# Tying the value and MoBA score matmuls of two heads, and their transposes, into runs

## Chip, core and metric

The kernel runs on one core of a Trainium2 chip. The metric is device microseconds of one execution, as the median of several runs. Times below are in microseconds (us) unless marked ns.

## What is computed

A trunk of two layers over 256 tokens of width 1024. Each layer normalises and modulates its input, projects it, runs eight MoBA heads and eight NSA heads (64 wide each), gates them, projects back and adds the result. With 256 tokens, one MoBA block covers the whole sequence and every NSA block is selected, so a MoBA head is one causal attention and an NSA head is the sum of two (selected and window branch) and a small compressed one.

```python
# MoBA, for each head: own block only
s_own = einsum('hqd,hkd->hqk', q, k_own); s_own = where(d_own >= 0, s_own - slope*d_own, NEG)
p = softmax(s_own); o_m = einsum('hqb,hbd->hqd', p, v_own)
# NSA, for each head: three gated branches
o_n = g0 * softmax(s_c) @ vc + g1 * softmax(s_s) @ vs + g2 * softmax(s_w) @ vw
y = concat([o_m * silu(zm), o_n * silu(zn)]) @ w_out
```

## The kernel before

**Projections.** TensorE (PE) multiplies float32 in split form: VectorE (DVE) and ScalarE (ACT) turn each 128x1024 unit of weights into a high part (`split_hi`, the `hi` cast of L364) and a low part (`split_lo`, the `lo` subtraction of L372), and `mm3` (L399 to L401) issues three matmuls per product. These are the bulk of PE's work; most have 256 columns and use the whole 128x128 array. Raw units come by DMA on SyncE's (SP) queue into a pool `raw` of eight slots, and a slot is free again when its `lo` is done.

**Attention.** Work goes by blocks of two heads (j = 0, 1), four NSA and four MoBA blocks a layer. Each has scores on PE, `softmax` on DVE and ACT (bias and minimum L545, exponential L548, reciprocal L550, a scaling per span at L555 on ACT or L557 on DVE), three transposes of 128x128 per head and branch (`transposed`, L565), a copy of the transposes out of PSUM (`PT`, L570 on ACT or L568 on DVE), the value matmuls, and `gate_out`.

- `nsa_block`: per head two score tiles (L586, L587), four spans; then six transposes, branch by branch (i = 0 selected, 1 window). The value sums of both heads stand in one PSUM bank `av`, head 0 on partitions 0 to 63, head 1 on 64 to 127, so each value matmul uses all 128 rows of the array and 64 of its columns: `vx` by `pct` for the compressed branch (L596), 256 columns of queries for the first key tile (L602), 128 for the second (L604).
- `moba_block`: per head the scores of the first query tile (128x128, L615) and of the second (128x256, L617). They contract over 64 partitions, head 0 on rows 0 to 63 of the array, head 1 on rows 64 to 127, into one `sc` bank each. Value matmuls at L627 (256) and L630 (128).

A float32 matmul that is not split shows as two records in the trace, each over the same columns; a transpose shows as one.

**What sets the order.** `PLAN` lists the steps; a scheduler then orders each engine's instructions by readiness and by the place in the program, so that projection matmuls of later steps fill PE while a softmax is under way. Nothing in the program before says that two matmuls should stand next to each other. The start of the first layer (up to about 56 us) has its order written by hand.

**Pools.** `raw` 8 slots, `work` 3 (the probability tiles `S` come from it), `probT` 3 (the `PT` copies); PSUM banks `tr` 2 (transposes), `sc` 2 (scores), `av` 1.

Of the kernel before, what the change touches and what calls it, by code (L numbers as in the profile page):

```python
# [41 lines left out]
# The first layer's modulation and first projections: (first row block, number) of each stage.  # L42
STAGES = [(0, 1), (1, 1), (2, 2), (4, 2), (6, 2)]
# Per stage, the engine that rounds its first weights to float32r: 1 ScalarE, 2 VectorE.
HIGH_ENGINE = (1, 2, 2, 1, 1)
# Per stage, the units of the next stage's modulation summed on VectorE (the rest on TensorE).
ON_VECTOR = (0, 0, 2, 2)
# Per stage, the column blocks of its projection before which parts of the next stage's
# modulation go: (units on TensorE), sums, columns.
ADA_AT = [((1, 1), 2, 3), ((0, 0, 2, 2), 2, 3), ((6, 6), 6, 6), ((2, 5), 5, 6)]  # L50
# Matmuls that keep the array's clock up before and after silu(c) and before the projections.
WARM = (1, 13, 6)

# Order of the steps: layer, kind, index, and after a colon choices of engines:
# p: modulation on TensorE; d: high parts of weights on VectorE; t: one of two copies of
# transposed probabilities on VectorE; v, s: normalisation on VectorE, ScalarE only.
# [12 lines left out]
class Trunk:  # L69
    def __init__(self, tc, ins, out):  # L70
        self.tc = tc
        self.nc = tc.nc
        self.I = ins
        self.out = out
        self.depth = ins["w_ada"].shape[0]
        self.n = 0
        self.how = ""
        self.used = set()
        self.parts, self.pv, self.z = {}, {}, [None, None]
# [12 lines left out]
    # ---------------------------------------------------------------- setup  # L92
# [64 lines left out]
    def silu_c(self):  # L157
        """silu(c) as columns, and each as the first of 32 columns (the others zero)."""
        nc = self.nc
        pc = self.tl(self.ps, [P, 512], "tr", bufs=2)  # L160
        nc.tensor.transpose(pc[:, :KK], self.c8, self.ident[:KK, :KK])
        th = self.cp.tile([P, KK], F32, name="cth")
        nc.scalar.activation(th, pc[:, :KK], AF.Tanh, scale=0.5)
        self.cs = self.cp.tile([P, KK], F32, name="cs")
        nc.vector.scalar_tensor_tensor(out=self.cs, in0=th, scalar=1.0, in1=pc[:, :KK],
                                       op0=OP.add, op1=OP.mult)
        nc.vector.tensor_scalar_mul(self.cs, self.cs, 0.5)
        nc.vector.tensor_copy(self.csz[:, :, 0], self.cs)

    # ------------------------------------------------------------------ ada  # L170
# [6 lines left out]
    def mod_rows(self, bank=("tr", 2)):  # L177
        """Columns of b_ada (+1 on the scale part), g_pre and g_post of a layer."""
# [9 lines left out]
    def ada_loads(self, l, spec, slots=None):  # L188
        """Weights of 512 columns of the modulation; spec lists (part, first kk, n kk)."""
# [14 lines left out]
    def ada_on_pe(self, pm, spec, i, raw, done=0):  # L204
        """Unit i of a group: each column block sums over d on its own 32 array columns
        (a single block of each part on two of them, for even and odd row blocks)."""
# [41 lines left out]
    def ada_cols(self, spec, ev):  # L248
        """The sums as columns of self.mod, with the bias and the norm's weight."""
# [29 lines left out]
    def warm(self, n):  # L279
        """Matmuls whose result nobody reads, to keep the array's clock up."""  # L280
# [4 lines left out]
    def gate_rows(self):  # L285
        """The gate part as rows, the same on every partition (through DRAM)."""
# [11 lines left out]
    # -------------------------------------------------------------- helpers  # L298
    def rstd(self, a, b):
        """(sum of the two mean-square parts + eps) ** -0.5."""  # L300
# [48 lines left out]
    def load(self, pieces, nk, n):  # L349
        """DMA of column pieces side by side into one unit."""  # L350
# [25 lines left out]
    def split(self, unit, tags=None):  # L376
        """The two f32r parts of a unit (in slots of self.mp if tags are given)."""
        return self.split_lo(unit, self.split_hi(unit, tags), tags)
# [4 lines left out]
    def weights(self, w, cols, tags=()):  # L383
        """Both f32r parts of the columns, a list over the 8 row blocks."""
# [11 lines left out]
    def mm3(self, out, aH, aL, bH, bL, first, last):  # L396
        """out (+)= a.T @ b from f32r parts: low terms first."""
# [14 lines left out]
    def col_chunk(self, l, cols, evac, t=None):  # L412
        """A chunk with the weights stationary; for one token tile at a time if t is given."""
# [14 lines left out]
    # ----------------------------------------------------------- compression  # L428
    def compress_in(self, l, pj):
        """The key and value columns by place within a block, and the place embeddings."""  # L430
# [105 lines left out]
    # ------------------------------------------------------------- attention  # L536
    def softmax(self, sc, h, spans, w):
        """Normalised (and gated) probabilities of the score spans of one bank."""
# [14 lines left out]
        for i, (a, b) in enumerate(spans):  # L553
            if b - a > P and "v" not in self.how or "s" in self.how:
                nc.scalar.activation(s[:, a:b], s[:, a:b], AF.Copy, scale=sm[:, i:i + 1])  # L555
            else:
                nc.vector.tensor_scalar_mul(s[:, a:b], s[:, a:b], sm[:, i:i + 1])  # L557
        return s

    def transposed(self, blocks, alt):  # L560
        """Transposes of the three causal probability blocks of one head and branch."""
        nc = self.nc
        pt = self.tl(self.ps, [P, 512], "tr", bufs=2)
        for i, blk in enumerate(blocks):
            nc.tensor.transpose(pt[:, i * P:(i + 1) * P], blk, self.ident)  # L565
        ps = self.tl(self.pp, [P, 3 * P], "PT")
        if alt and "t" in self.how:
            nc.vector.tensor_copy(ps, pt[:, :3 * P])  # L568
        else:
            nc.scalar.copy(ps, pt[:, :3 * P])  # L570
        return ps

    def nsa_block(self, b):
# [3 lines left out]
        pts = []  # L577
        for j in range(2):
            h = 2 * b + j
            s01 = []  # L580
            for qt in range(NT):
# [8 lines left out]
            pts.append([self.transposed([s01[0][:, i * P:(i + 1) * P],  # L590
                                         s01[1][:, i * S:i * S + P],
                                         s01[1][:, i * S + P:(i + 1) * S]], i)
                        for i in range(2)])
        for j in range(2):
            h = 2 * b + j
            nc.tensor.matmul(av[j * HD:(j + 1) * HD, :S], self.vx[:, h, :], self.pct,  # L596
                             start=True, stop=False)
        for i in range(2):
            for j in range(2):
                o = av[j * HD:(j + 1) * HD, :]  # L600
                vc = slice(i * P + g * HD, i * P + (g + 1) * HD)
                nc.tensor.matmul(o[:, :S], self.vsw[:, 0, vc], pts[j][i][:, :S],  # L602
                                 start=False, stop=False)
                nc.tensor.matmul(o[:, P:S], self.vsw[:, 1, vc], pts[j][i][:, S:],  # L604
                                 start=False, stop=(i == 1))
        self.gate_out(av, 4 + b)

    def moba_block(self, b):
        nc = self.nc
        av = self.tl(self.ps, [P, 512], "av", bufs=1)  # L610
        pts = []
        for j in range(2):
            rows = slice(j * HD, (j + 1) * HD)
            sc = self.tl(self.ps, [P, 512], "sc", bufs=2)
            nc.tensor.matmul(sc[:, 0:P], self.qm[rows, b, 0:P], self.km[rows, b, 0:P],  # L615
                             start=True, stop=True)
            nc.tensor.matmul(sc[:, P:3 * P], self.qm[rows, b, P:S], self.km[rows, b, :],  # L617
                             start=True, stop=True)
            s = self.softmax(sc, 2 * b + j, [(0, P), (P, 3 * P)], None)
            pts.append(self.transposed([s[:, i * P:(i + 1) * P] for i in range(3)], j))  # L620
        for kt in range(2):
            for j in range(2):
                h = 2 * b + j
                o = av[j * HD:(j + 1) * HD, :]
                vc = slice(h * HD, (h + 1) * HD)
                if kt == 0:
                    nc.tensor.matmul(o[:, :S], self.vm[:, 0, vc], pts[j][:, :S],  # L627
                                     start=True, stop=False)
                else:
                    nc.tensor.matmul(o[:, P:S], self.vm[:, 1, vc], pts[j][:, S:],  # L630
                                     start=False, stop=True)
# [11 lines left out]
    # ---------------------------------------------------------------- output  # L643
# [8 lines left out]
    def out_mm(self, t):  # L652
        """Pieces (columns, bank) of y @ w_out for a token tile."""
# [43 lines left out]
    # ------------------------------------------------------------- evacuation  # L697
# [10 lines left out]
    def ev_k(self, pj):  # L708
        """High and low parts of the keys of both branches, on both halves of the partitions."""
# [16 lines left out]
    def ev_qn(self, i):  # L726
        """The NSA queries whole, and per head as high and low parts on the two halves."""
# [29 lines left out]
    # ------------------------------------------------------------------ layer  # L757
# [16 lines left out]
    def first_layer_start(self):  # L774
        """Modulation, h and the first projections, some of the 8 row blocks at a time."""
# [140 lines left out]
    def first(self, name, l):  # L916
        """Whether this is the first use of a tile in a layer."""
# [4 lines left out]
    def step(self, token):  # L922
        """One step of PLAN: layer, kind, index and, after a colon, engine choices."""
# [71 lines left out]
    def run(self):  # L995
        from contextlib import ExitStack
        with ExitStack() as self.stack:
            self.cp = self.pool("const")
            self.rp = self.pool("raw", bufs=8)
# [3 lines left out]
            self.wp = self.pool("work", bufs=3)  # L1003
            self.pp = self.pool("probT", bufs=3)
# [28 lines left out]
```

## Time and profile before

| | us |
|---|---|
| median of 3 runs | 355.85 |
| lowest and highest run | 354.7, 356.37 |
| span of the profiled execution | 354.4 |
| PE busy (96% of the span), 2852 matmul records | 341.4 |
| PEld (weight loads) | 299.6 |
| DVE busy (75%) | 266.1 |
| ACT busy (58%) | 204.3 |
| POOL | 10.5 |

The span of 354.4 is the one time that the profile has for its own execution; the runs' median is 1.45 above it. PE's busy time counts each matmul from its start to its modelled end, and these overlap: what a matmul holds PE for is read from its start to the start of the next. A projection matmul of 256 columns has a duration of 0.28 and its successor starts 0.12 after it. The granted clock of PE is 1.00 (2.4 GHz) in every stretch that matters here.

### The profile page before, as it was taken

What the parts mean: (1) busy time and instruction counts of PE and PEld (TensorE: products, weight loads), DVE (VectorE), ACT (ScalarE), POOL (GpSimd) and SP (SyncE); (2) the same over time, 40 slices, a digit from 0 to 9 for tenths busy, and PEclk for the clock granted to TensorE, in tenths of its full rate; (3) what the DMA queues carried; (4) which work ended last, traced back from release to release, by engine and by line L of the source; (5) the groups of instructions that cost most, each with busy time, mean ns of one, the idle gap of its engine ahead of it and who ended that gap; (6) DMA issues with size and microseconds to landing.
All of it is one profiled execution on the core that took longest, in us unless ns stands there. A gap on an engine that the chain in (4) does not pass through costs nothing.

```text
span 354.4 us, 7595 instructions
## 1 busy us (share of the span) xinstructions
PE 341.4 (96%) x2852; PEld 299.6 (85%) x2852; DVE 266.1 (75%) x727; ACT 204.3 (58%) x506; POOL 10.5 (3%) x23
## 2 busy tenths in 40 slices
PE   7999999999999999989999999999999999999993
PEld 7789889988887878767998999998878898677993
DVE  2648669999987898879898985999987646776132
ACT  4423407776989863757365455543889655668211
POOL 2000001100000000000011000000000000000000
PEclk9999999999999999999999999999999999999998
DMA  7999999939955566899755798489454330000111
GB/s 237 321 331 353 350 338 220 308 108 354 347 186 154 167 217 210 259 351 333 197 149 162 223 284 247 130 285 352 130 160 139 119 120 2 0 2 1 62 60 59
DMA packets 72060, 71.12 MB, mean 201 GB/s; under 512 B 11440, under 2 KB 61784, under 8 KB 72024
## 3 DMA queue, kind: packets, MB, share of 16 engines
q1 hardware_dynamic: 72024, 70.65, 64.1%
q8 instruction: 22, 0.36, 0.4%
q14 instruction: 14, 0.11, 0.1%
HBM read 69.58 MB, written 1.06 MB: 199 GB/s over the span
## 4 chain that ended last, share of the span: by engine, by line
PE 73%; DVE 13%; DMA 6%; issue 4%; ACT 2%; POOL 1%; SPq 1%; DVEq 0%; POOLq 0%; ACTq 0%
PE pj L399 13%; PE pj L400 13%; PE pj L401 13%; PE tr L565 5%; DVE lo L372 4%; PE av L602 3%; PE tr L216 3%; DMA yL<-in_w_ada_dram 2%; DMA raw<-in_w_out_dram 2%; PE av L627 2%; PE sc L586 2%; PE sc L617 2%; PE av L604 2%; PE pj L839 2%; PE av L596 2%
## 5 line engine op out<-in xcount | busy, mean ns | idle before, releaser
L372 DVE TENSOR_TENSOR lo<-raw,hi 128x1024 fp32r<-128x1024 f32 (+3 forms) x82 | 90.7, 1123 | 15.9 <-ACT hi L364 15.5
L399 PE MATMUL pj<-hH,lo 128*128 128x256 f32 x320 | 93.1, 291 | 0.0
L400 PE MATMUL pj<-hL,hi 128*128 128x256 f32 x320 | 92.5, 289 | 0.0
L401 PE MATMUL pj<-hH,hi 128*128 128x256 f32 x320 | 92.1, 288 | 0.0
L364 ACT CAST hi<-raw 128x1024 fp32r<-128x1024 f32 (+4 forms) x70 | 66.0, 966 | 22.7 <-PE pj L401 17.1
L399 PEld LDWEIGHTS pj<-hH,lo 128*128 128x128 f32 x320 | 61.0, 191 | 4.4 <-issue 3.4
L400 PEld LDWEIGHTS pj<-hL,hi 128*128 128x128 f32 x320 | 61.0, 191 | 2.2 <-issue 1.7
L401 PEld LDWEIGHTS pj<-hH,hi 128*128 128x128 f32 x320 | 61.0, 191 | 1.4 <-issue 1.1
L548 ACT ACTIVATE S<-S,mn 128x128 f32<-128x128 f32 (+1 forms) x96 | 42.7, 448 | 4.4 <-DVE mn L545 4.1
L233 DVE SCALAR_TENSOR_TENSOR acc<-raw,cs,acc 128x512 f32<-128x512 f32 x49 | 36.5, 747 | 1.6 <-DMA raw<-in_w_ada_dram 1.2
L545 DVE CUSTOM_DVE_ANT_0 S<-sc,bias 128x128 f32<-128x128 f32 (+1 forms) x96 | 31.6, 350 | 7.6 <-PE tr L565 3.1
L399 PE MATMUL pj<-hi,yL 128*128 128x256 f32 x112 | 31.9, 285 | 0.0
L401 PE MATMUL pj<-hi,yH 128*128 128x256 f32 x112 | 31.9, 286 | 0.0
L400 PE MATMUL pj<-lo,yH 128*128 128x256 f32 x112 | 31.8, 285 | 0.0
L565 PE MATMUL tr<-ident,S 128*128 128x128 f32 x144 | 29.6, 281 | 0.0
L570 ACT COPY PT<-tr 128x384 f32<-128x384 f32 x44 | 20.3, 478 | 10.0 <-PE tr L565 9.9
L565 PEld LDWEIGHTS tr<-ident,S 128*128 128x128 f32 x144 | 17.5, 140 | 6.7 <-issue 3.0
L555 ACT ACTIVATE S<-S,sm 128x256 f32<-128x256 f32 (+1 forms) x46 | 20.4, 483 | 2.9 <-DVE sm L550 1.4
L399 PEld LDWEIGHTS pj<-hi,yL 128*128 128x128 f32 x112 | 21.2, 189 | 0.9 <-issue 0.9
L401 PEld LDWEIGHTS pj<-hi,yH 128*128 128x128 f32 x112 | 21.1, 189 | 0.5 <-issue 0.5
L400 PEld LDWEIGHTS pj<-lo,yH 128*128 128x128 f32 x112 | 21.0, 188 | 0.3 <-issue 0.3
L548 ACT ACTIVATION_READ_ACCUMULATOR S<-S,mn 128x1 f32 x96 | 18.3, 190 | 0.0
(248 smaller groups left out, 650.1 us busy)
## 6 DMA issues: line engine op xcount, KB each, us to landing
raw<-in_w_in_dram SPq DMA_DIRECT2D x43, 512.0 KB, 4.5
raw<-in_w_ada_dram SPq DMA_DIRECT2D x32, 512.0 KB, 4.6
raw<-in_w_out_dram SPq DMA_DIRECT2D x16, 512.0 KB, 7.2
raw<-in_w_in_dram SPq DMA_DIRECT2D x9, 256.0 KB, 3.9
qs<-in_w_ada_dram SPq DMA_DIRECT2D x4, 512.0 KB, 7.2
yH<-in_w_ada_dram SPq DMA_DIRECT2D x4, 512.0 KB, 7.2
yL<-in_w_ada_dram SPq DMA_DIRECT2D x4, 512.0 KB
raw<-in_w_in_dram SPq DMA_DIRECT2D x9, 128.0 KB, 5.7
```

The costliest lines, as they stand in the source:

```text
L216: self.nc.tensor.matmul(pm[32 * r:32 * r + 32, :P], self.csz[:, k, :], raw[:, j, c * P:(c + 1) * P], start=first <= k < first + turns, sto ...
L233: nc.vector.scalar_tensor_tensor(out=out, in0=raw[:, j], scalar=self.cs[:, k:k + 1], in1=out, op0=OP.mult, op1=OP.add)
L364: self.nc.scalar.copy(hi[:, :nk * n], raw[:, :nk * n])
L372: self.nc.vector.tensor_sub(lo[:, :nk * n], raw[:, :nk * n], hi[:, :nk * n].bitcast(F32))
L399: nc.tensor.matmul(out, aL, bH, start=first, stop=False)
L400: nc.tensor.matmul(out, aH, bL, start=False, stop=False)
L401: nc.tensor.matmul(out, aH, bH, start=False, stop=last)
L545: nc.vector.tensor_tensor_reduce(out=s[:, a:b], in0=sc[:, a:b], in1=self.bias[:, h, S - (b - a):S], scale=-1.0, scalar=3.0e38, op0=OP.add, ...
L548: nc.scalar.activation(s[:, a:b], s[:, a:b], AF.Exp, bias=mn[:, i:i + 1], scale=-1.0, accum_out=sm[:, i:i + 1])
L555: nc.scalar.activation(s[:, a:b], s[:, a:b], AF.Copy, scale=sm[:, i:i + 1])
L565: nc.tensor.transpose(pt[:, i * P:(i + 1) * P], blk, self.ident)
L570: nc.scalar.copy(ps, pt[:, :3 * P])
```

## The change

The change touches only `softmax` (it now remembers its last instructions), `transposed`, `nsa_block`, `moba_block`, three pool sizes, and comments.

- A new helper `beside` gives every matmul of a list a wait on all instructions of a second list, and puts an order among the matmuls.
- The transposes of one branch of both heads are one list of six, and all six wait for the scalings of both heads (in an NSA block the eight scalings of the branch's spans are `scaled[i::2]`, four for each branch).
- The value matmuls of a branch are one list in the order head 0, head 1, head 0, head 1, and wait for both `PT` copies. In the selected branch the two `vx` matmuls stand at the head of the list.
- The four MoBA score matmuls of a block are one list in the order head 0, head 1 for 128 columns, then both for 256; the list waits for nothing more.
- `raw` has seven slots, `work` four, `probT` four.

```diff
-    def transposed(self, blocks, alt):
...
+    def transposed(self, pair, after):
+        nc = self.nc
+        mms, pts = [], []
+        for j, blocks in enumerate(pair):
+            pt = self.tl(self.ps, [P, 512], "tr", bufs=2)
+            mms += [nc.tensor.transpose(pt[:, i * P:(i + 1) * P], blk, self.ident)
+                    for i, blk in enumerate(blocks)]
+            ps = self.tl(self.pp, [P, 3 * P], "PT")
...
+        self.beside(mms, after)
+        return pts
+    def beside(self, mms, lasts):
+        for mm in mms:
+            for last in lasts:
+                self.tc.add_manual_dep(mm.ins, last.ins.name, mybir.DependencyInfo(
+                    mybir.DependencyClass.Sync, mybir.DependencyReason.DATA), reason="beside")
+        for a, b in zip(mms, mms[1:]):
+            self.tc.add_manual_dep(b.ins, a.ins.name, mybir.DependencyInfo(
+                mybir.DependencyClass.NoSync, mybir.DependencyReason.DATA), reason="order")
     def nsa_block(self, b):
...
+        scaled = self.scaled[-8:]
         for i in range(2):
+            pts = self.transposed([[s01[0][:, i * P:(i + 1) * P],
+                                    s01[1][:, i * S:i * S + P],
+                                    s01[1][:, i * S + P:(i + 1) * S]] for s01 in probs],
+                                  scaled[i::2])
+            mms = []
+            if i == 0:
+                mms += [nc.tensor.matmul(av[j * HD:(j + 1) * HD, :S], self.vx[:, 2 * b + j, :],
+                                         self.pct, start=True, stop=False) for j in range(2)]
...
+            for kt in range(2):
+                for j in range(2):
+                    mms.append(nc.tensor.matmul(
+                        av[j * HD:(j + 1) * HD, kt * P:S], self.vsw[:, kt, vc],
+                        pts[j][:, kt * S:S + kt * P], start=False, stop=(i == 1 and kt == 1)))
+            self.beside(mms, self.copies[-2:])
     def moba_block(self, b):
...
+        sc = [self.tl(self.ps, [P, 512], "sc", bufs=2) for _ in range(2)]
+        mms = []
+        for qt in range(2):
+            for j in range(2):
+                rows = slice(j * HD, (j + 1) * HD)
+                mms.append(nc.tensor.matmul(
+                    sc[j][:, qt * P:P + qt * S], self.qm[rows, b, qt * P:(qt + 1) * P],
+                    self.km[rows, b, :(qt + 1) * P], start=True, stop=True))
+        self.beside(mms[::1], [])
+        ss = [self.softmax(sc[j], 2 * b + j, [(0, P), (P, 3 * P)], None) for j in range(2)]
+        pts = self.transposed([[s[:, i * P:(i + 1) * P] for i in range(3)] for s in ss],
+                              self.scaled[-4:])
...
-            self.rp = self.pool("raw", bufs=8)
+            self.rp = self.pool("raw", bufs=7)
...
-            self.wp = self.pool("work", bufs=3)
-            self.pp = self.pool("probT", bufs=3)
+            self.wp = self.pool("work", bufs=4)
+            self.pp = self.pool("probT", bufs=4)
```

**How the order moves, place 1.** PE, the value matmuls of the second NSA block of layer 0. Before, they stand in four groups, of which the last three follow here; head 0 has `PT_1278` and `PT_1284` (selected and window branch), head 1 `PT_1318` and `PT_1324`.

```order
L565 MATMUL tr_1314<-ident,S_1289 128x128
L602 MATMUL av_1245<-PT_1278,vsw_169 64x256
L565 MATMUL tr_1320<-ident,S_1289 128x128
L604 MATMUL av_1245<-PT_1278,vsw_169 64x128
...
L602 MATMUL av_1245<-PT_1318,vsw_169 64x256
L604 MATMUL av_1245<-PT_1318,vsw_169 64x128
L602 MATMUL av_1245<-PT_1284,vsw_169 64x256
L604 MATMUL av_1245<-PT_1284,vsw_169 64x128
L602 MATMUL av_1245<-PT_1324,vsw_169 64x256
L604 MATMUL av_1245<-PT_1324,vsw_169 64x128
```

The same block with the change (selected branch; `PT_1306` is head 0, `PT_1312` head 1):

```order
L569 MATMUL tr_1302<-ident,S_1263 128x128 x2
L569 MATMUL tr_1308<-ident,S_1277 128x128
L569 MATMUL tr_1308<-ident,S_1291 128x128 x2
L402 MATMUL pj_1669<-hH_167,hi_1665 128x256
L569 MATMUL tr_1320<-ident,S_1249 128x128
L569 MATMUL tr_1320<-ident,S_1263 128x128 x2
L400 MATMUL pj_1784<-hH_167,lo_1776 128x256
L617 MATMUL av_1245<-pct_1076,vx_1049 64x256 x2
L622 MATMUL av_1245<-PT_1306,vsw_169 64x256
L622 MATMUL av_1245<-PT_1312,vsw_169 64x256
L622 MATMUL av_1245<-PT_1306,vsw_169 64x128
L622 MATMUL av_1245<-PT_1312,vsw_169 64x128
```

The ten value matmuls of a block go from four groups to two of six and four, heads alternating; between a branch's transposes and its value matmuls only a few other matmuls are left.

**Place 2.** PE, MoBA scores of layer 1, near the end of the NSA blocks. Before (`sc_4097` is head 1 of the first MoBA block, `sc_4125` and `sc_4144` the two heads of the second):

```order
L615 MATMUL sc_4097<-km_3546,qm_3545 128x128
L565 MATMUL tr_4051<-ident,S_4026 128x128
L602 MATMUL av_3982<-PT_4015,vsw_2460 64x256
...
L617 MATMUL sc_4097<-km_3546,qm_3545 128x256
L615 MATMUL sc_4125<-km_3546,qm_3545 128x128
...
L617 MATMUL sc_4125<-km_3546,qm_3545 128x256
...
L615 MATMUL sc_4144<-km_3546,qm_3545 128x128
L617 MATMUL sc_4144<-km_3546,qm_3545 128x256
```

Now (`sc_4125` and `sc_4126` are the two heads of the second block):

```order
L636 MATMUL sc_4125<-km_3546,qm_3545 128x128
L636 MATMUL sc_4126<-km_3546,qm_3545 128x128
L636 MATMUL sc_4125<-km_3546,qm_3545 128x256
L636 MATMUL sc_4126<-km_3546,qm_3545 128x256
L622 MATMUL av_3982<-PT_4061,vsw_2460 64x256
L622 MATMUL av_3982<-PT_4067,vsw_2460 64x256
L622 MATMUL av_3982<-PT_4061,vsw_2460 64x128
L622 MATMUL av_3982<-PT_4067,vsw_2460 64x128
```

The four scores of a block stand together here and in the third block of layer 1. In five of the other six blocks the first of the four still stands alone, with 1 to 9 other matmuls behind it; in the sixth the last one does. Before, layer 0 had all four scores of a block next to each other in each of its blocks, head after head; layer 1 had its sixteen scores in eleven groups.

**Place 3.** ACT, from the copies of the second NSA block's selected branch to those of the third, with the change:

```order
L575 COPY PT_1306<-tr_1302 128x384
L575 COPY PT_1312<-tr_1308 128x384
...
L575 COPY PT_1330<-tr_1326 128x384
L365 CAST hi_1872<-raw_1870 128x1024
L557 ACTIVATE S_1484<-S_1484,sm_1486 128x256 x2
...
L549 ACTIVATE S_1512,sm_1514<-S_1512,mn_1513 128x256 x2
L365 CAST hi_1878<-raw_1876 128x1024
L557 ACTIVATE S_1512<-S_1512,sm_1514 128x256 x2
L575 COPY PT_1527<-tr_1523 128x384
```

`S_1484` belongs to head 0 and `S_1512` to head 1 of the third block; the six transposes behind `PT_1527` wait for both now, and a `hi` cast stands ahead of the last scaling. Before, the transposes of head 0 waited for `S_1484` alone.

## Rows read from the trace of the kernel before

**Rows 1.** The page, chain that ended last, shares of the span by engine.

```profile
PE 73%; DVE 13%; DMA 6%; issue 4%; ACT 2%; POOL 1%; SPq 1%; DVEq 0%; POOLq 0%; ACTq 0%
```

**Rows 2.** Stages: us; busy (x instructions) of PE, PEld, DVE, ACT, POOL; clock; DMA.

```profile
94.00:134.00 40.00, 40.00 (x296) 31.70 (x293) 34.41 (x129) 32.42 (x97) 0.00 (x0) 1.00 0.63 196
...
243.00:280.00 37.00, 37.00 (x280) 30.15 (x280) 29.94 (x114) 29.95 (x88) 0.00 (x0) 1.00 0.50 165
296.00:330.00 34.00, 34.00 (x228) 24.48 (x226) 23.35 (x100) 23.71 (x75) 0.00 (x0) 1.00 0.01 1
```

**Rows 3.** Timeline of PE: start, duration, line, operands, records; value matmuls, layer 0.

```profile
101.47 0.28 PE L399 MATMUL pj<-hH,lo 128*128 128x256 f32 x1
101.68 0.66 PE L602 MATMUL av<-PT,vsw 128*64 128x256 f32 x4
102.16 0.40 PE L604 MATMUL av<-PT,vsw 128*64 128x128 f32 x4
102.38 0.59 PE L602 MATMUL av<-PT,vsw 128*64 128x256 f32 x2
102.81 0.38 PE L604 MATMUL av<-PT,vsw 128*64 128x128 f32 x2
103.12 0.44 PE L565 MATMUL tr<-ident,S 128*128 128x128 f32 x2
```

**Rows 4.** Timeline of PE: first groups of value matmuls of the second NSA block.

```profile
104.68 0.65 PE L596 MATMUL av<-pct,vx 128*64 128x256 f32 x4
105.26 0.39 PE L399 MATMUL pj<-hH,lo 128*128 128x256 f32 x1
105.48 0.28 PE L400 MATMUL pj<-hL,hi 128*128 128x256 f32 x1
105.60 0.27 PE L401 MATMUL pj<-hH,hi 128*128 128x256 f32 x1
...
107.56 0.65 PE L602 MATMUL av<-PT,vsw 128*64 128x256 f32 x2
108.13 0.33 PE L565 MATMUL tr<-ident,S 128*128 128x128 f32 x1
108.39 0.43 PE L604 MATMUL av<-PT,vsw 128*64 128x128 f32 x2
108.75 0.38 PE L586 MATMUL sc<-wide,qs 128*128 128x256 f32 x1
```

**Rows 5.** Timeline of PE: first group of value matmuls of a MoBA block.

```profile
162.53 0.65 PE L627 MATMUL av<-PT,vm 128*64 128x256 f32 x2
163.10 0.39 PE L399 MATMUL pj<-hi,yL 128*128 128x256 f32 x1
```

**Rows 6.** Timeline of PE: MoBA scores, both heads (139), one head (320).

```profile
139.27 0.50 PE L615 MATMUL sc<-km,qm 64*128 64x128 f32 x4
...
140.13 0.39 PE L399 MATMUL pj<-hH,lo 128*128 128x256 f32 x1
...
320.56 0.49 PE L615 MATMUL sc<-km,qm 64*128 64x128 f32 x2
320.88 0.59 PE L617 MATMUL sc<-km,qm 64*128 64x256 f32 x2
321.41 0.39 PE L401 MATMUL pj<-hi,yH 128*128 128x256 f32 x1
```

**Rows 7.** Timeline of PE: the last value matmuls of the kernel.

```profile
329.16 0.81 PE L627 MATMUL av<-PT,vm 128*64 128x256 f32 x4
...
330.11 0.27 PE L289 MATMUL tr<-ident,mod 128*8 128x128 f32 x1
```

**Rows 8.** Groups by line and shape, ACT: busy us, mean ns; idle before, releaser.

```profile
L364 ACT CAST hi<-raw 128x1024 fp32r<-128x1024 f32 x56 | 57.9, 1050 | 22.7 <-PE pj L401 17.1 <-issue 2.8 <-DMA raw<-in_w_out_dram 1.6
L570 ACT COPY PT<-tr 128x384 f32<-128x384 f32 x44 | 20.3, 478 | 10.0 <-PE tr L565 9.9
```

**Rows 9.** Waits of SP's queue: us in total, times, longest.

```profile
SPq L356 <- DVE lo L372: 56.7, 26, 8.4
```

More of the change, by code (lines that the diff above doesn't have):

```diff
@@ L78, in __init__ @@
         self.used = set()
+        self.copies, self.scaled = [], []
         self.parts, self.pv, self.z = {}, {}, [None, None]
@@ L554, in softmax @@
             if b - a > P and "v" not in self.how or "s" in self.how:
-                nc.scalar.activation(s[:, a:b], s[:, a:b], AF.Copy, scale=sm[:, i:i + 1])
-            else:
-                nc.vector.tensor_scalar_mul(s[:, a:b], s[:, a:b], sm[:, i:i + 1])
+                self.scaled.append(
+                    nc.scalar.activation(s[:, a:b], s[:, a:b], AF.Copy, scale=sm[:, i:i + 1]))
+            else:
+                self.scaled.append(
+                    nc.vector.tensor_scalar_mul(s[:, a:b], s[:, a:b], sm[:, i:i + 1]))
         return s
-    def transposed(self, blocks, alt):
+    def transposed(self, pair, after):
         nc = self.nc
[L563 to L571, printed above, removed]
+        mms, pts = [], []
[4 more added lines that the diff above has]
+            ps = self.tl(self.pp, [P, 3 * P], "PT")
+            if j and "t" in self.how:
+                self.copies.append(nc.vector.tensor_copy(ps, pt[:, :3 * P]))
+            else:
+                self.copies.append(nc.scalar.copy(ps, pt[:, :3 * P]))
+            pts.append(ps)
+        self.beside(mms, after)
[8 more added lines that the diff above has]
+                mybir.DependencyClass.NoSync, mybir.DependencyReason.DATA), reason="order")
     def nsa_block(self, b):
@@ L576, in nsa_block @@
         av = self.tl(self.ps, [P, 512], "av", bufs=1)
-        pts = []
+        probs = []
         for j in range(2):
@@ L589, in nsa_block @@
                                         self.gate[:, qt, 3 * h + 1:3 * h + 3]))
[L590 to L597, printed above, removed]
-        for i in range(2):
[L599 to L605, printed above, removed]
+            probs.append(s01)
+        scaled = self.scaled[-8:]
+        for i in range(2):
+            pts = self.transposed([[s01[0][:, i * P:(i + 1) * P],
[6 more added lines that the diff above has]
+                                         self.pct, start=True, stop=False) for j in range(2)]
+            vc = slice(i * P + g * HD, i * P + (g + 1) * HD)
+            for kt in range(2):
[4 more added lines that the diff above has]
+            self.beside(mms, self.copies[-2:])
         self.gate_out(av, 4 + b)
@@ L610, in moba_block @@
         av = self.tl(self.ps, [P, 512], "av", bufs=1)
[L611 to L620, printed above, removed]
+        sc = [self.tl(self.ps, [P, 512], "sc", bufs=2) for _ in range(2)]
[10 more added lines that the diff above has]
+                              self.scaled[-4:])
+        mms = []
         for kt in range(2):
@@ L623, in moba_block @@
                 h = 2 * b + j
[L624 to L631, printed above, removed]
+                mms.append(nc.tensor.matmul(
+                    av[j * HD:(j + 1) * HD, kt * P:S], self.vm[:, kt, h * HD:(h + 1) * HD],
+                    pts[j][:, kt * S:S + kt * P], start=(kt == 0), stop=(kt == 1)))
+        self.beside(mms, self.copies[-2:])
         self.gate_out(av, b)
```

## The prediction, made before the changed kernel ran

> **What bounds the kernel now.** I read the page first, then the stages, then PE's timeline inside the attention blocks, then ACT's groups and the waits of SP's queue. The chain that ended last gives PE 73% of the span and DVE 13% [rows 1], so time that PE no longer needs should mostly come back. The stages say where that may fail: in 94 to 134 (the NSA blocks of layer 0) DVE is busy for 34.41 of 40 us and ACT for 32.42; in the NSA blocks of layer 1 each has about 30 of 37; in the last MoBA blocks some 23.5 of 34 [rows 2]. Everywhere PE shows as full and its clock as 1.00, so the busy share cannot tell useful columns from drain. For that I read starts: what a matmul holds PE for is the distance to the next start.
>
> **What a value matmul costs today.** Heads 0 and 1 use different column halves of the array. Four records of 256 columns, two heads, take 102.16 - 101.68 = 0.48; one head's two take 102.81 - 102.38 = 0.43 [rows 3]. Two neighbours of different heads thus cost hardly more than one. The same for 128 columns: a pair takes 0.22, and one head 0.31 with the step back to the full array behind it, so that step costs 0.31 - 0.22 = 0.09 [rows 3]. The step in: the projection matmul ahead of the run holds PE for 101.68 - 101.47 = 0.21 [rows 3], where two projection matmuls in peace stand 105.60 - 105.48 = 0.12 apart, so 0.09 too; and the first projection matmul after a run has its successor after 105.48 - 105.26 = 0.22, so 0.10 more [rows 4] (a transpose in that place about 0.055, an estimate at half, its 128 columns being half of 256). An excursion into half-array matmuls so costs 0.09 + 0.09 + 0.10 = 0.28 beside its passes, and its first pass of a pair 0.05 more than a later one (0.48 against 0.43).
>
> **NSA value matmuls, before.** The first group, `vx` of both heads: 0.58 to the next start, 0.09 in, 0.10 behind: 0.77. Head 0's 256 columns alone: 108.13 - 107.56 = 0.57, and 0.09 in: 0.66. The transpose behind it holds PE for 0.26, of which 0.15 is drain; head 0's 128 columns alone take 108.75 - 108.39 = 0.36, and 0.10 behind: 0.61 together [rows 4]. The last six: 103.12 - 101.68 = 1.44 with the step back, 0.09 in, 0.055 behind: 1.59 [rows 3]. A block: 3.6. **After**: the run of six is 0.48 (`vx` pair) + 0.43 + 0.22 and 0.24 of steps (a transpose behind), 1.37; the run of four 0.48 + 0.22 + 0.28 = 0.98. Together 2.35, so 1.25 less. Three of the eight blocks already have one more overlap today; I give them 0.95. Sum: 5 x 1.25 + 3 x 0.95 = **9.1**.
>
> **MoBA value matmuls.** Today head 0's 256 columns are an excursion of their own, 0.57 + 0.09 + 0.10 = 0.76 [rows 5], and the other three overlap to about the run of four, 0.98. Tied, the 0.76 goes: 7 x 0.76 = **5.3**. The last block has its four together already, with 0.95 from the first to the transpose behind [rows 7]: nothing.
>
> **MoBA scores.** These pair by row halves. Both heads' four take 140.13 - 139.27 = 0.86, and 0.19 of steps (0.09 in, 0.10 behind): 1.05; one head's two take 321.41 - 320.56 = 0.85, also 1.04 with steps; a lone 128 is 320.88 - 320.56 = 0.32 and 0.28: 0.60; a lone 256 about 0.8 (0.53 and 0.28) [rows 6]. Layer 0 stands well today (two blocks at 1.05; in the other two the heads overlap in part, and I take 1.5, halfway from 1.05 to twice 1.04: 5.2 with rounding). The tie puts an order on the four but keeps nothing out between them, and in five of eight blocks the first stands alone with other work behind it: 0.60 and 1.04 for the three left. Layer 0 goes to about 6.8, **1.6 lost**. Layer 1 goes from eleven excursions (eight heads at 1.04 and three more steps of 0.28 make 9.2; I take 8.6 for what little overlaps) to two blocks at 1.0 (joined to value runs) and two at 1.6: 5.2, **3.4 won**.
>
> **Transposes.** They use the whole array, so six in a row or three and three cost the same; priced at nothing for PE. The tie's price is its wait, below.
>
> Gross: 9.1 + 5.3 - 1.6 + 3.4 = **16.2 us**.
>
> **What is given back.** (1) Value matmuls now wait for both copies. From the last transpose's start to the copy's end is 0.27 (a transpose [rows 7]) + 0.478 (the copy [rows 8]), and 0.1 for PE to see it, an estimate of one projection matmul: 0.85. The order leaves two or three projection matmuls and three transposes there, 2 x 0.12 + 3 x 0.11 = 0.57. So 0.3 for each selected branch, 2.4 over eight blocks, and some 0.9 for the MoBA blocks, where fillers are more: **3.3**. Bounds: nothing, where the scheduler has more to fill with, and 16 branches at 0.85 = 13.6 if it has nothing. I take the order's rows. (2) In 94 to 134, PE's gain (about half of 9.1) asks DVE and ACT for the same work in less time: DVE at 34.41 would have to stand above 0.95 of what is left, where waits for each other begin. I give half of the stage's gain and some more back: **2.6** (bounds 0 and 4.5). (3) `raw` with seven slots: SP waits on `lo` for 56.7 us in 26 waits, up to 8.4 each [rows 9]; a slot less means the same transfers start one unit later. Behind the start of the kernel, weights arrive well ahead, since DMA is busy 0.63 and 0.50 in the NSA stages [rows 2]; in the start itself the last unit of a stage now waits for a `lo` that is done before its DMA is issued. **0.3**; from above one longest wait, 8.4; from below, nothing. (4) `work` and `probT` at four: each can only take a wait away, and two heads' tiles must live together now; nothing.
>
> Net: 16.2 - 3.3 - 2.6 - 0.3 = 10.0 us, off the span of 354.4: 344.4. The median stands 1.45 above that span, so **345.9**.
>
> **A rule against the change.** The value pair in [rows 3] shows two heads' matmuls in 0.48 where one takes 0.43. The Trainium skill, page "TensorE: Matmul & The Clock Gate", section "Part 3: Packing small matmuls — row/col tiling", has weight loads overlap matmuls in flight only where their row groups differ; value matmuls share all 128 rows, so by it heads could not overlap and neighbours would queue. By it the sum would be the third rival's, a loss. The row of this trace disagrees, so that rival gets a small chance.
>
> **The rivals.**
>
> - *ACT and DVE become the bound.* For it: DVE at 34.41 of 40, ACT at 32.42 [rows 2], and ties that bind two heads to the later one. Against it: 13% for DVE in the chain [rows 1], and MoBA stages with a third of their time free. If both NSA stages give back their whole 9.1 (2.6 of it is in the sum already), the gain is 10.0 - 6.5 = 3.5: **352.4**, range 349.5 to 354.
> - *Slower: the tie of the six transposes.* Head 0's transposes now wait for head 1's last scaling, and on ACT a `hi` cast of 1.05 us [rows 8] stands ahead of it (place 3). If PE has run out of fillers there, each of 16 ties (eight blocks, two branches) waits for the cast, and for about 0.48 of scaling behind it (by the copy's row, of near shape): 1.5 x 16 = 24 against 16.2 won: 355.85 + 7.8 = **363.7**. It decides from 16.2 / 16 = 1.0 us a tie. Against it: with the change head 0's transposes have more projection matmuls ahead in PE's order, so fillers cover most of it.
> - *Value pairs don't overlap.* Then the block loses what pairs win: the NSA blocks save only excursions. Ten value matmuls of a block one by one are 6 x 0.43 + 4 x 0.22 and 0.56 of steps, 4.0 against 3.6: 0.4 lost, over eight blocks 3.2; MoBA 2 x 0.43 + 2 x 0.22 + 0.28 = 1.58 against 1.74, 1.1 won; scores 1.8 won. -3.2 + 1.1 + 1.8 = -0.3, less 3.3 + 0.3 of waits: 3.9 slower, **359.8**. The pair in [rows 3] speaks against it.
> - *Nothing to measure.* A measurement of this kernel can tell about 0.5%, 1.8 us, from no change. The change would end there if 16.2 were nearly all given back: waits of 0.85 at all branches (13.6) with the 2.6 of the NSA stage do just that: **355.9**.
>
> **How the numbers follow.** Forecast 0.64 (340 to 349.5: 16.2 kept but for a few waits, or 10 us of it lost); DVE and ACT as the bound 0.20; the transposes' tie 0.07; no overlap 0.03; nothing 0.06. Faster is 0.64 + 0.20 = 0.84, same 0.06, slower 0.10. The range 340.0 to 354.0 holds the first two cases; what it leaves out is the other three, 0.16.
>
> **What the changed profile would show.** Right: runs of value matmuls, all records of two heads within 0.48 for 256 columns; PE's excursions down from four to two in an NSA block; the NSA stage of layer 0 shorter by 2 us or more, the last MoBA block no shorter; DVE's share of the chain up from 13%. Wrong: idle of PE of over 0.85 ahead of `vx` or a copy-waiting value matmul; idle of PE ahead of the first of six transposes, released by a scaling; a new wait of SP on `lo` that lets a projection wait for its weights; or pairs whose second head starts only after the first's end, 0.43 later.

## The result, and the profile after

The changed kernel takes **342.55 us** (median of 4 runs, 342.16 to 344.3) beside 355.37 of the kernel before: ratio 0.9648, 95% interval 0.9612 to 0.9684, faster by 12.8 us. 345.9 was predicted, in a range of 340 to 354. The profiled execution, the slowest of the four (344.3), has a span of 342.6, 11.8 less than that of before.

The page of the changed kernel, PE's busy time and the chain by engine (beside [rows 1]):

```profile
PE 327.5 (96%) x2852; PEld 294.5 (86%) x2852; DVE 264.8 (77%) x727; ACT 203.0 (59%) x506; POOL 10.2 (3%) x23
...
PE 68%; DVE 15%; DMA 8%; issue 4%; ACT 2%; POOL 1%; SPq 1%; DVEq 0%; POOLq 0%; ACTq 0%
```

The stages, with the columns of [rows 2]:

```profile
94.00:134.00 40.00, 39.86 (x325) 34.18 (x323) 36.42 (x127) 32.71 (x97) 0.00 (x0) 1.00 0.68 215
...
243.00:280.00 37.00, 37.00 (x306) 32.71 (x306) 31.66 (x113) 32.53 (x92) 0.00 (x0) 1.00 0.57 187
...
296.00:330.00 34.00, 33.67 (x285) 28.75 (x285) 20.15 (x78) 20.39 (x63) 0.55 (x1) 1.00 0.09 32
```

PE is as busy as before, but holds 325 records where it held 296 in 94 to 134, and 306 where it held 280 in 243 to 280. DVE rises to 36.42 of 40 us and does not hold PE up.

PE's timeline in the second NSA block of layer 0, start, duration, line, operands, records (beside [rows 3, 4]):

```profile
109.26 0.82 PE L569 MATMUL tr<-ident,S 128*128 128x128 f32 x6
109.84 0.36 PE L402 MATMUL pj<-hH,hi 128*128 128x256 f32 x1
110.32 0.55 PE L569 MATMUL tr<-ident,S 128*128 128x128 f32 x3
110.63 0.36 PE L400 MATMUL pj<-hH,lo 128*128 128x256 f32 x1
110.92 0.65 PE L617 MATMUL av<-pct,vx 128*64 128x256 f32 x4
111.40 0.82 PE L622 MATMUL av<-PT,vsw 128*64 128x256 f32 x8
112.15 0.55 PE L569 MATMUL tr<-ident,S 128*128 128x128 f32 x3
...
113.79 0.87 PE L622 MATMUL av<-PT,vsw 128*64 128x256 f32 x8
114.59 0.39 PE L604 MATMUL sc<-wide,qs 128*128 128x256 f32 x1
```

(A row's form is that of its first record: the eight records hold both widths.) The run of six lasts 112.15 - 110.92 = 1.23, the run of four 114.59 - 113.79 = 0.80; the prediction had 0.48 + 0.43 + 0.22 and 0.48 + 0.22, each with 0.09 out: 1.22 and 0.79. All eight blocks of the trace repeat these two lengths to 0.01.

The MoBA scores of the first and the third block of layer 1 (beside [rows 6]):

```profile
293.20 0.49 PE L636 MATMUL sc<-km,qm 64*128 64x128 f32 x2
293.62 0.38 PE L401 MATMUL pj<-hL,hi 128*128 128x256 f32 x1
...
294.88 0.92 PE L636 MATMUL sc<-km,qm 64*128 64x128 f32 x6
295.73 0.39 PE L401 MATMUL pj<-hL,hi 128*128 128x256 f32 x1
...
304.50 0.93 PE L636 MATMUL sc<-km,qm 64*128 64x128 f32 x8
305.68 0.87 PE L647 MATMUL av<-PT,vm 128*64 128x256 f32 x8 [0.26 <-DVE PT L573]
```

The first block's first score runs off alone (0.42 to the next start) and the other three come 1.7 us later, as the order had it; the third block's four stand whole, and the values behind them wait 0.26 for a copy.

**Where PE's time went.** For each profiled execution I took every matmul's distance to the next start and put it down by kind: values and scores of MoBA with up to 0.15 of drain on the matmul ahead and the one behind; a transpose of probabilities at 0.028 if a projection matmul follows, at 0.109 otherwise (why, below); a projection matmul of 256 columns at 0.118, which is in "rest" with all other kinds; what is left over is "waits". A projection matmul right behind a transpose holds PE for 0.20 (also below), so 0.08 of each such place stands in "waits": these two columns are read together. Some 7.5 us at the two ends of a span (8.7 in tr_free) stand in no column.

| kernel (span of its profile) | values | scores | transposes | waits | rest |
|---|---|---|---|---|---|
| before (354.4) | 39.7 | 13.3 | 12.4 | 13.8 | 267.7 |
| changed (342.6) | 25.9 | 11.4 | 14.9 | 14.8 | 268.0 |
| changed, once more: after_again (344.8) | 25.9 | 12.2 | 14.9 | 16.4 | 267.8 |
| v_head (347.6) | 29.9 | 11.7 | 14.9 | 15.3 | 268.4 |
| v_nowait (355.1) | 37.0 | 11.6 | 14.5 | 14.6 | 269.6 |
| v_only (344.5) | 23.7 | 15.8 | 12.8 | 17.7 | 266.9 |
| ten (342.0) | 22.8 | 13.7 | 14.5 | 14.8 | 268.6 |
| tr_free (346.9) | 26.3 | 14.2 | 12.9 | 15.1 | 269.7 |
| sc_free (342.5) | 25.9 | 11.5 | 14.8 | 14.6 | 268.1 |
| sc_tog (339.0) | 25.9 | 9.1 | 14.9 | 13.4 | 268.2 |
| sc_tog_again (339.4) | 25.9 | 9.1 | 14.9 | 13.0 | 269.0 |
| before_raw7 (355.3) | 40.0 | 13.8 | 12.4 | 12.8 | 268.8 |
| before_work4 (356.9) | 42.5 | 13.4 | 13.2 | 13.1 | 267.2 |
| before_pools (360.0) | 42.5 | 13.5 | 13.2 | 15.6 | 267.7 |

Values give 13.8, scores 1.9; transposes and waits together take back 3.5, the rest 0.3: 11.9 of 11.8. Two executions of one kernel differ by up to 1.6 in waits, so nothing under 2 us is read from the waits of one. That 1.6 is after_again's, whose granted clock was 0.50 (1.2 GHz) from 155 to 161, after PE had been busy for 0.00 us of 151 to 152 and 0.53 of 152 to 153; the first profile has 1.00 there.

### The profile page after: what moved, and what is told of

It is laid out like the page before. It is cut to its first block, busy times and chain, and to the rows that moved or that the text cites. A ratio compares the mean times of both kernels' runs of the same rounds, so it can differ in the third digit from the quotient of the medians.

```text
span 342.6 us, 7585 instructions
## 1 busy us (share of the span) xinstructions
PE 327.5 (96%) x2852; PEld 294.5 (86%) x2852; DVE 264.8 (77%) x727; ACT 203.0 (59%) x506; POOL 10.2 (3%) x23
## 4 chain that ended last, share of the span: by engine, by line
PE 68%; DVE 15%; DMA 8%; issue 4%; ACT 2%; POOL 1%; SPq 1%; DVEq 0%; POOLq 0%; ACTq 0%
PE pj L400 14%; PE pj L401 13%; PE pj L402 13%; PE tr L569 5%; DVE lo L373 4%; PE av L622 3%; DMA yL<-in_w_ada_dram 3%; PE tr L217 2%; PE sc L636 2%; DMA km<-in_w_ada_dram 2%; PE sc L604 2%; PE sc L605 2%; PE pj L858 2%; PE av L647 2%; DMA raw<-in_w_in_dram 2%
## 5 line engine op out<-in xcount | busy, mean ns | idle before, releaser
L373 DVE TENSOR_TENSOR lo<-raw,hi 128x1024 fp32r<-128x1024 f32 (+3 forms) x82 | 90.6, 1124 | 14.1 <-ACT hi L365 13.8
L401 PE MATMUL pj<-hL,hi 128*128 128x256 f32 x320 | 91.4, 286 | 0.0
L365 ACT CAST hi<-raw 128x1024 fp32r<-128x1024 f32 (+4 forms) x70 | 66.2, 966 | 18.3 <-PE pj L402 15.6
L546 DVE CUSTOM_DVE_ANT_0 S<-sc,bias 128x128 f32<-128x128 f32 (+1 forms) x96 | 30.9, 350 | 4.4 <-PE tr L569 2.6
L575 ACT COPY PT<-tr 128x384 f32<-128x384 f32 x44 | 19.9, 480 | 12.8 <-PE tr L569 12.5
L569 PE MATMUL tr<-ident,S 128*128 128x128 f32 x144 | 21.9, 278 | 0.2
L246 ACT COPY accr<-tr 128x128 f32<-128x128 f32 x12 | 3.2, 265 | 25.4 <-PE tr L241 18.4
```

What stands on the lines that cost most here:

```text
L365: self.nc.scalar.copy(hi[:, :nk * n], raw[:, :nk * n])
L373: self.nc.vector.tensor_sub(lo[:, :nk * n], raw[:, :nk * n], hi[:, :nk * n].bitcast(F32))
L401: nc.tensor.matmul(out, aH, bL, start=False, stop=False)
L546: nc.vector.tensor_tensor_reduce(out=s[:, a:b], in0=sc[:, a:b], in1=self.bias[:, h, S - (b - a):S], scale=-1.0, scalar=3.0e38, op0=OP.add, ...
L569: mms += [nc.tensor.transpose(pt[:, i * P:(i + 1) * P], blk, self.ident) for i, blk in enumerate(blocks)]
L575: self.copies.append(nc.scalar.copy(ps, pt[:, :3 * P]))
```

## The experiments

**Is it overlap, or only fewer steps in and out?** v_head keeps runs, waits and excursions, and writes the values of a run head after head.

```diff
-            for kt in range(2):
-                for j in range(2):
+            for j in range(2):
+                if i == 0:
+                    mms.append(nc.tensor.matmul(av[j * HD:(j + 1) * HD, :S], self.vx[:, 2 * b + j, :], self.pct, start=True, stop=False))
+                for kt in range(2):
```

(The pair of `vx` ahead of it goes, and `moba_block` swaps its loops likewise.)

> The changed kernel, with the value matmuls of a run written head after head (vx, 256, 128 columns of head 0, then those of head 1); runs, waits, number of excursions stay. If the pairs of two heads overlap (two heads' 256 columns in 0.48, one head's in 0.43): a run of six takes 0.48 + 0.43 + 0.43 + 0.43 + 0.22 + 0.09 = 2.08 in place of 1.23, a run of four 1.22 in place of 0.80, so 8 x 0.85 + 16 x 0.42 = 13.5 us more: 356, no faster than the kernel before. Rival, the gain is only the steps in and out of half-array matmuls: 342.6, as the changed kernel.

350.12, ratio to the kernel before 0.9846 (0.98 to 0.9893), so neither: clearly slower than the changed kernel, but by about half of the 13.5 expected. The trace of v_head, first NSA block, same columns:

```profile
100.53 0.65 PE L619 MATMUL av<-pct,vx 128*64 128x256 f32 x2
101.01 0.38 PE L623 MATMUL av<-PT,vsw 128*64 128x256 f32 x1
101.02 0.43 PE L619 MATMUL av<-pct,vx 128*64 128x256 f32 x1
101.23 0.38 PE L623 MATMUL av<-PT,vsw 128*64 128x256 f32 x1
101.28 0.38 PE L619 MATMUL av<-pct,vx 128*64 128x256 f32 x1
101.44 0.87 PE L623 MATMUL av<-PT,vsw 128*64 128x128 f32 x6
102.24 0.44 PE L569 MATMUL tr<-ident,S 128*128 128x128 f32 x2
```

In the program these six stand as

```
L619 MATMUL av_1150<-pct_1076,vx_1049 64x256
L623 MATMUL av_1150<-PT_1211,vsw_169 64x256
L623 MATMUL av_1150<-PT_1211,vsw_169 64x128
L619 MATMUL av_1150<-pct_1076,vx_1049 64x256
L623 MATMUL av_1150<-PT_1217,vsw_169 64x256
L623 MATMUL av_1150<-PT_1217,vsw_169 64x128
```

Head 1's `vx` starts at 101.02, beside head 0's 256 columns and 0.42 ahead of head 0's 128, which stand before it in the program. So PE started a later matmul early here, on the other column half, and a run written head after head still overlaps in part: the six take 102.24 - 100.53 = 1.71 in place of 1.23, and the four 0.81 in place of 0.80 in each of the blocks. 8 x 0.48 = 3.8 is the 4.0 of the table. (The spans differ by 5.0 and the medians by 6 to 7.5; 4.0 of it is in the values, and the rest is not shown to come from the order. Part of it is the clock: in v_head's profile the granted clock was 0.50 (1.2 GHz) from 156 to 159, after PE had been busy for 0.21 us of 154 to 155.) That overlap counts is shown; that the heads must alternate strictly is not so.

**Is it the order, or the wait?** v_nowait keeps the order of the list and drops its wait for both copies.

```diff
-            self.beside(mms, self.copies[-2:])
+            self.beside(mms, [])
```

> The changed kernel with the order of the value matmuls kept and their wait for both copies left out (each waits for its own copy, as its data need). Its order has 36 runs of value matmuls in place of 24. If the common wait is what keeps the pairs together: 12 more steps in and out, 12 x 0.28 = 3.4 us, and some lone passes, 1 to 2: 347 to 349. If the wait costs the 3.3 us that the prediction gave it and the order alone does the rest: 342 to 343.

354.6, ratio 0.998 (0.9953 to 1.0008): **the whole gain is gone.** Values stand at 37.0, 11.1 above the changed kernel, the rest is within the spread. By the prediction's price the 12 more excursions are 3.4 of it. Another 5.8 stands in the 20 runs that still hold four in the right order: they take 21.8 where 20 runs of 0.80 take 16.0. The other 1.9 stays open. One of the 20, in the first NSA block of v_nowait:

```profile
103.91 1.11 PE L622 MATMUL av<-PT,vsw 128*64 128x256 f32 x8
104.94 0.39 PE L605 MATMUL sc<-wide,qs 128*128 128x256 f32 x1
```

1.03 for what takes 0.80 in the changed kernel: the second head starts later by its copy and the heads end up staggered. Waits of the weight loads on the copies (us in total, times, longest), first v_nowait, then the changed kernel:

```profile
PEld av L622 <- ACT PT L575: 3.7, 18, 0.3
```

```profile
PEld tr L569 <- ACT PT L575: 1.2, 5, 0.3
PEld av L617 <- ACT PT L575: 0.8, 5, 0.2
PEld av L622 <- ACT PT L575: 0.8, 3, 0.3
```

The wait looks like a cost and is what buys the gain: with it other work fills the time until both heads are ready. Without it the `vx` pair goes alone in all eight NSA blocks, one head goes ahead alone in four other places, and 19 of the 20 runs of four are longer than 0.80. A run with the common wait and no order among the matmuls was not made.

**Values alone, and a longer run.** v_only puts the value lists, with their waits, into the kernel before (with the three pool sizes); all ten of an NSA block fall into one run. ten makes that one list in the changed kernel, behind all twelve transposes of the block; of its edit the wait is shown:

```diff
-            self.beside(mms, self.copies[-2:])
+        self.beside(mms, self.copies[-4:])
```

> The kernel before with the three pool sizes and the value matmuls tied and waiting for both copies; transposes and scores as before. Its order has the ten of an NSA block in one run (16 runs in all, in place of 44): values 8 x 2.0 + 8 x 0.98 = 24 us where the trace of before has 41.6, 17.6 less; scores in 20 groups in place of 15, 1.4 more; pools 3.6 more: 343.5. If the tie of the transposes is needed for the gain, as the run without it suggests (347.4): 347 or more. If the values were not the gain: 355 or more.

> The changed kernel with all ten value matmuls of an NSA block in one run that waits for all four copies: 16 runs in place of 24. Eight steps in and out less, 8 x (0.28 + 0.05) = 2.6 us; but its order cuts the scores into 19 groups in place of 14, 5 x 0.28 = 1.4 more: 341.4. If the wait for the last copy shows on PE (up to 0.85 for each of eight blocks): 344 to 348.

v_only: 347.94, ratio 0.9775 (0.9715 to 0.9835): faster than before, and 4 to 5 us short of the changed kernel, as its second theory had it. The values did what was expected (23.7), but scores went to 15.8; transposes and waits together are 0.8 above the changed kernel's. ten: 344.64, ratio 0.9659 (0.9627 to 0.9691), the same as the changed kernel: in the profiles 3.1 won on values, 2.3 lost on scores that its order cut into more groups, and 0.2 on the rest.

**The tie of the transposes.**

```diff
-        self.beside(mms, after)
         return pts
```

> The changed kernel without the tie of the six transposes (neither the wait for both heads' scalings nor the order). If six in a row cost PE nothing, as predicted, and the wait is covered: 342.6. If a transpose with a projection matmul behind it is cheaper (0.028 to the next start) than one with a transpose behind it (0.109), as starts in both traces suggest: 30 fewer transposes with a transpose behind, 30 x 0.08 = 2.4 us faster, 340.2, and up to 1 us more if the tie's wait shows too.

347.43, ratio 0.9760 (0.9711 to 0.9809): slower, where both theories had no change or a gain. The 2.0 less in "transposes" is no gain, since the matmul behind each pays it back (below). Scores cost 2.8 more, since transposes that come ready one head at a time stand among them (18 groups in place of 14). The 1.7 more in "rest" lie mostly ahead of the attention, where the edit changes nothing: in this execution the granted clock was 0.50 (1.2 GHz) from 77 to 79, after PE had been busy for 0.23 us of 75 to 76, where the changed kernel's first profile has 1.00 behind a gap of like length. Two of the four runs, this one among them, have mean clocks of 0.989 and 0.988 and take 348.7 and 348.8; the other two (0.997 and 0.995) take 346.2 and 346.1, beside 342.2 to 344.3 for the changed kernel at 0.994 to 0.998. So the tie is worth some 2 to 4 us. Most of it is likely the scores, which v_only cuts up too; the split is not settled.

**The scores.** sc_free writes them head after head without an order, as before; sc_tog makes all four wait for the same two minima.

```diff
-        self.beside(mms[::1], [])
+        self.beside(mms, self.mins[-2:])
```

(`softmax` appends its last minimum to `self.mins`.)

> The changed kernel with the MoBA scores written head after head and without an order among them, as before. By the sum of the prediction the order lost 1.6 us in layer 0 and won 3.4 in layer 1, so 344.4 without it. By its order (thirteen groups, four of them whole) it loses less in layer 1 than before: 342 to 343. If both heads' scores gain nothing from standing together: 342.6.

> The changed kernel in which all four MoBA scores of a block also wait for the last minima of the two softmaxes ahead, so that none runs off alone: by its order six blocks have their four together and two have one and three. Sum by the rows: 6 x 1.05 + 2 x 1.64 = 9.6 us of scores where the changed kernel's trace has 12.2: 2.6 faster, 340. If the time is set by ACT and DVE there, or the later first score holds the block up: 342.6 or more.

sc_free: 344.57, ratio 0.9692 (0.9635 to 0.9749), no difference to the changed kernel; scores 11.5 against 11.4. Without the order layer 0 spends 1.0 less on them and layer 1 1.2 more: in sum the order without a wait brings nothing. sc_tog: **341.48**, ratio 0.9575 (0.9549 to 0.9601). Its first block of layer 1, where the changed kernel took 0.42 and 0.85:

```profile
291.71 0.93 PE L637 MATMUL sc<-km,qm 64*128 64x128 f32 x8
292.56 0.39 PE L400 MATMUL pj<-hH,lo 128*128 128x256 f32 x1
```

Six of eight blocks stand like this, scores fall to 9.1. It beats both kernels; to see by how much, it ran once more beside the changed one.

> The changed kernel as it is, on the same chip as the runs beside it, so that small differences can be read: 342.6 to 344 (0.9648 of the kernel before).

> The scores kept together once more, beside the changed kernel on one chip. By the sum of starts on PE (9.1 us of scores in place of 11.4, waits 1.5 less) 2.5 to 3.5 faster than the changed kernel. If the first difference came from another chip, or another day of it: no difference.

After_again 344.11, ratio 0.9673 (0.9622 to 0.9723); sc_tog_again 341.46, 0.9606 (0.957 to 0.9642). 2.6 us between the medians, as expected, the scores again 9.1; the two intervals overlap a little, while those of the first comparison do not.

**The pools.** In the kernel before: all three sizes, `raw` 7 alone, `raw` 7 and `work` 4.

```diff
-            self.rp = self.pool("raw", bufs=8)
+            self.rp = self.pool("raw", bufs=7)
-            self.wp = self.pool("work", bufs=3)
+            self.wp = self.pool("work", bufs=4)
-            self.pp = self.pool("probT", bufs=3)
+            self.pp = self.pool("probT", bufs=4)
```

> The kernel before with the three pool sizes of the change alone (raw 7, work 4, probT 4). By the prediction: 0.3 us slower, 355.7, with nothing to measure. Rival, that part of the gain is buffers and not ties: 350 to 353. Rival, that a raw slot is dear: 358 or more.

> The kernel before with seven slots of raw alone. The three pool sizes together cost it 3.6 us (1.0109). If the slot of raw is what costs, 359; if it is what four slots of work and probT do to the order (47 runs of value matmuls in place of 44), 355.4 to 356.2 here.

> The kernel before with raw 7 and work 4. Raw alone gave 1.0017, all three pools 1.0109. If the fourth slot of work is what costs (its order has 47 runs of value matmuls, as with all three pools, where before has 44): 359.5. If probT is: 356.9.

All three: 359.72, 1.0109 (1.0059 to 1.0158). `raw` alone: 356.93, 1.0017 (0.9997 to 1.0037). `raw` and `work`: 358.7, 1.0081 (1.0046 to 1.0116). The slot of `raw` is cheap; the fourth slot of `work` costs the kernel before 2 to 3 us. It takes away a wait, and with it the scheduler forms 47 runs of values in place of 44 (values 42.5 in place of 39.7). Another buffer can so be a loss where the order follows readiness. In the changed kernel the ties set the runs; `work` at three was not timed there, since four tiles of two heads must live together.

## Why the prediction was right

Direction, range and the mechanism of the gain were right. The terms of what is given back mostly were not, and their errors partly cancel. Step by step:

- **Value runs.** 9.1 + 5.3 = 14.4 predicted, 13.8 by the table. The lengths of 1.22 and 0.79 came out as 1.23 and 0.80 in all 24 runs of the changed kernel.
- **Scores.** -1.6 and +3.4, in sum 1.8; the table has 1.9 (by layers 1.9 lost and 3.5 won, if all of the drain behind them is counted). By sc_free about 1.0 of the loss and 1.2 of the gain are the order's, the rest comes with the other ties.
- **Transposes.** "Priced at nothing for PE" held, though the table's column goes from 12.4 to 14.9. Before, they stood mostly in ones and twos with other matmuls behind. Two places of the trace of before, PE's timeline:

```profile
106.17 0.27 PE L565 MATMUL tr<-ident,S 128*128 128x128 f32 x1
106.20 0.48 PE L587 MATMUL sc<-wide,qs 128*128 128x512 f32 x1
106.52 0.38 PE L565 MATMUL tr<-ident,S 128*128 128x128 f32 x2
106.66 0.37 PE L400 MATMUL pj<-hL,hi 128*128 128x256 f32 x1
106.86 0.28 PE L401 MATMUL pj<-hH,hi 128*128 128x256 f32 x1
```

  From a transpose to the next start it is 0.03 if a full matmul follows (106.20 - 106.17) and 0.11 if a transpose does (106.66 - 106.52 = 0.14 for two). But what the first saves, the matmul behind it pays: 106.86 - 106.66 = 0.20, where two projection matmuls in peace stand 0.12 apart. Over the trace of before, a projection matmul with a transpose ahead and another projection matmul behind holds PE for 0.202 (median of 39), one between two projection matmuls for 0.120 (1156). A transpose and a projection matmul so take 0.23, by 0.03 + 0.20 or by 0.11 + 0.12. With the change 115 transposes have a transpose behind them in place of 70, and 21 a projection matmul in place of 52; that moves 2.5 us from "waits" to "transposes" and costs PE nothing.
- **Give-back (1), waits for both copies:** 3.3 predicted. The two rows of NSA values that wait on `PT` above sum to 1.6 with the change, and to 0.7 in before:

```profile
PEld tr L565 <- ACT PT L570: 0.8, 2, 0.4
...
PEld av L602 <- ACT PT L570: 0.7, 2, 0.4
```

  So some 0.9 more. The 0.3 for each branch was too much: eight waits of values for a copy are left over sixteen runs, 0.2 each. The row of `tr` (1.2, beside 0.8) is a wait that the prediction does not have: by the code, the window branch's transposes need a `tr` bank that the copy of the selected branch's frees. Waits in all, read with the transposes, rose by 3.5 in one profile and 5.1 in the other; not all of that is located.
- **Give-back (2), DVE and ACT in 94 to 134:** 2.6 predicted, and **this term failed**: no wait of PE for DVE is seen there. DVE went to 36.42 of 40 with PE still at 39.86. A share of 0.9 was no bound yet; the chain moved by 2% to DVE and by 2% to DMA, no more. DVE did take back 1.0 elsewhere, where the prediction looked for nothing: the first projection of layer 1 waits for the low part of its input, in both profiles of the changed kernel, where the longest such wait in before is 0.3.

```profile
PE pj L400 <- DVE hL L348: 1.0, 1, 1.0
```

  (`transposed` also lets DVE copy head 1's `PT` where it copied the window branch's, in the one NSA block whose step has a `t`; two of four copies either way.)
- **Give-back (3), `raw`:** 0.3 predicted, 0.6 (-0.1 to 1.3) measured by before_raw7. **(4), `work` and `probT`:** "nothing" failed in the kernel before (above).

The score sum has two slips: by its own terms layer 0 goes from 5.1 to 4 x 1.64 = 6.6, so 1.5 lost, not 1.6. So 16.2 gross was 15.7, and the 6.2 given back were 3.8. Of the two large terms one was too big and the other did not come, and waits that the sum does not have made up for part of them: errors that partly cancel. Of the 3.3 or so between 345.9 and 342.55 only 1.8 is in the spans (344.4 and 342.6). The other 1.5 is chance: the 1.45 stood for a median above the profiled span, and after the change the profiled execution was the slowest, so the median stands 0.05 below its span. The rival by which value pairs don't overlap would have given 359.8; v_head shows that overlap pays, and v_nowait that it does not come without the wait. The rule of the Trainium skill (page "TensorE: Matmul & The Clock Gate", section "Part 3: Packing small matmuls — row/col tiling") that weight loads overlap matmuls in flight only where row groups differ does not hold in these runs. Heads that share all 128 rows run side by side, two in 0.48 where one takes 0.43 ([rows 3], and every run of the changed kernel); in its first NSA block the eight weight loads for the `PT` matmuls run from 101.36 to 102.15, while matmuls that started from 101.09 on are in flight. The slower rival, the transposes' tie, went the other way: the tie is worth 2 to 4 us.

## What to carry to other kernels

Where two small matmuls can share the array, give both a wait on the later one's input: the change without this wait gained nothing here (354.6), with it 12.8 us. Read what a matmul costs from the distance to the next start, and look at the matmul behind it too before a price is set: the same transpose shows 0.03 or 0.11, but with the projection matmul beside it 0.23 both times. A step into half-array work and back cost 0.28. When buffers are added, look at the order that comes out, not only at the wait that goes.

## What was not expected of the chip

- PE started a matmul on the other column half 0.42 us ahead of one that stands before it in the program (v_head).
- From a transpose to a 256-column projection matmul behind it is 0.028, to another transpose 0.109 (52 and 70 such places in before), and the projection matmul then holds PE for 0.202 in place of 0.120: it makes up for the difference.
- Two heads whose operands come ready one after the other do not fall into step within the run: 1.03 in place of 0.80 for the same four matmuls.
